# A hybrid attention and convolution layer on one core: x, weights, w_out and gates laid out in DRAM in the pieces in which they are loaded

## Chip, cores and metric

The kernel runs on one core of one Trainium2 chip. The metric is the device time of one execution in microseconds (us), lower is better.

## What is computed

One layer is applied to two sequences, of 256 and 2,048 tokens, each with the same 16 learned meta tokens ahead of it; the outputs of the meta tokens are dropped. All tensors are float32. Cut to what matters:

```python
h = rmsnorm(z, norm_w)                                  # z: (B, 16 + S, 1024)
proj = einsum('bld,de->ble', h, w_in)                   # w_in: (1024, 2816)
q, k, v, g_att, c_val, c_glu, g_conv = split(proj, ...) # 512 128 128 512 512 512 512
q, k = rmsnorm per head of 64                           # 8 query heads, 2 key heads
att = windowed_gqa(q, k, v, sink) * silu(g_att)         # window 128, ALiBi, meta keys, sink logit
u   = c_val * sigmoid(c_glu)
cnv = silu(layernorm(depthwise_conv31(u) + conv_b)) * silu(g_conv)
out = z + einsum('ble,ed->bld', concat([att, cnv]), w_out)
```

## The kernel before

**Precision.** Products are made from split operands: each float32 tensor becomes a rounded part and a remainder (`xh`, `xl` for x, the two halves of `ws` for the weights), and three matrix products stand in for one (`PASSES`, used at L763, L779 and L538).

**First part: projections.** The 2,304 tokens are 18 blocks of 128 and lie with 16 meta columns in six groups (`GROUPS`: one of 400 columns, five of 384). w_in is cut into 11 units of 256 columns: four for the convolution (GLU gate beside value), two convolution gates, two attention gates, one for k and v, two for q. The units are run over groups 0 to 2 first and over groups 3 to 5 after that. For each group `Prep` loads x transposed (`load`, L649, from `zt`, in four pieces of two row blocks each into `xt`), scales it (`scale`, L677) and splits it (`split`, L694 and L703). The scale needs the reciprocal norms, which `stats` makes from rows of z (L626 load, L632 squares, L122 and L123 the power) and `first` turns into a row with transposes (`bc`, L661). For each unit `weights` loads w_in in four pieces of 256 KB (L729, tile `wraw`), splits them (L738, L739) into `ws`, and for units after the second writes the split halves to DRAM (`wd`, L742), from where the second pass loads them (L720).

**What goes through DRAM between the parts.** The gates after SiLU (L871, tile `go`, three buffers) go to `gd`, queries to `qd`, keys to `kd`, values to `vd`, the convolution's output (made on VectorE at L846, one tap per instruction, beside the projections) to `cd`. `store` issues a store two ticks after its tile was made; a tick ends each half unit of a group.

**Second part: attention and output projection.** The 18 blocks are run in a pipeline of three stages with eight slots each (`slot_step`): scores of block a (L316, the bias and running maximum at L371, the exponential at L383), probabilities transposed and multiplied with v (L429, L464) for the block before, output projection (L538) for the one before that. `load_ga` (L299) and `load_mix` (L303, L305) bring the attention gate, the convolution gate and the convolution's output of a block; `merge` (L499, L505) and `mix_conv` (L515) multiply. `load_wo` (L290) loads w_out in 16 pieces of 256 KB through two `woraw` buffers, and `split_wo` (L294 on ScalarE, L295 on VectorE) splits them. This happens in the change-over, while the last q unit is still being projected.

**Order.** Nearly all transfers are issued by SyncE's one queue, in order. The scheduler orders the first part by a time model; in the second part GpSimd's order, and later TensorE's too, is that of the code (`manual_schedule`, `keep_in_program_order`). Each engine works through its instructions in order, so a waiting instruction holds those behind it.

Of the kernel before, what the change touches and what calls it, by code (L numbers as in the profile page):

```python
# [10 lines left out]
F32 = mybir.dt.float32  # L11
# [6 lines left out]
P = 128  # L18
D = 1024
ND = D // P  # L20
# [3 lines left out]
NB = NB_P + NB_S  # L24
TOK = NB * P
COLS = NM + TOK
# [6 lines left out]
UW = 256  # L33
# [27 lines left out]
GROUPS = [(0, 400)] + [(400 + 384 * i, 384) for i in range(5)]  # L61
# [14 lines left out]
def hymba_kernel(  # L76
# [13 lines left out]
    nc = tc.nc  # L90

    const = ctx.enter_context(tc.tile_pool(name="const", bufs=1, side="left"))
    dram = ctx.enter_context(tc.tile_pool(name="dram", bufs=1, space=bass.MemoryType.DRAM))
    psum = ctx.enter_context(tc.tile_pool(name="psum", bufs=2, space=bass.MemoryType.PSUM))

    qd = dram.tile([NB, P, 512], F32, name="qd")
    gd = dram.tile([8, P, TOK], F32, name="gd")
    kd = dram.tile([P, 2, KV, TOK], F32, name="kd")
    kmd = dram.tile([P, 2, KV, NM], F32, name="kmd")
    vd = dram.tile([NB, P, 2 * P], F32, name="vd")  # L100
# [35 lines left out]
    def later(k, f):  # L136
        due.setdefault(clock[0] + k, []).append(f)
# [20 lines left out]
    def store(dst, src):  # L158
        later(2, lambda: nc.sync.dma_start(dst, src))
# [53 lines left out]
    vt, qt, q2t, sbt, pmt, gat, gct, cnt, mix, att, yot, opj = ({} for _ in range(12))  # L213
# [45 lines left out]
    vt, qt, q2t, sbt, pmt, gat, gct, cnt, mix, att, yot, opj = ({} for _ in range(12))  # L259
# [17 lines left out]
    def load_wo(n):  # L277

        e = OUT_ORDER[n]
        for hl in range(2):  # L280
            idx = 2 * n + hl
            if idx % 3 == 0:
                slot = idx // 3
                wo_slot[slot] = xp.tile([P, ND, 400], F32R, tag=("xh", "xl")[slot % 2], name=f"wo{slot}")
            flat = wo_slot[idx // 3].rearrange("p a n -> p (a n)")
            wo[e, hl] = flat[:, D * (idx % 3) : D * (idx % 3) + D]
        for nh in range(2):
            cols = slice(512 * nh, 512 * nh + 512)
            raw = pool["a"].tile([P, 512], F32, tag="woraw", name=f"woraw{n}_{nh}", bufs=2)
            nc.sync.dma_start(raw, w_out[e][:, cols])  # L290
            later(2, lambda hi=wo[e, 0][:, cols], lo=wo[e, 1][:, cols], raw=raw: split_wo(hi, lo, raw))

    def split_wo(hi, lo, raw):
        nc.scalar.copy(hi, raw)  # L294
        nc.vector.tensor_tensor(lo, raw, hi, op=ALU.subtract)  # L295

    def load_ga(b):
        gat[b] = pool["b"].tile([P, 4, P], F32, tag="ga", name=f"ga{b}", bufs=1)
        nc.sync.dma_start(gat[b], gd[0:4, :, P * b : P * b + P].rearrange("j p n -> p j n"))  # L299

    def load_mix(b):
        gct[b] = pool["b"].tile([P, 4, P], F32, tag="gc", name=f"gc{b}")
        nc.sync.dma_start(gct[b], gd[4:8, :, P * b : P * b + P].rearrange("j p n -> p j n"))  # L303
        cnt[b] = pool["b"].tile([P, 4, P], F32, tag="cn", name=f"cn{b}")
        nc.sync.dma_start(cnt[b].rearrange("p j n -> p (j n)"), cd[b])  # L305

# [311 lines left out]
    if True:  # L618
# [20 lines left out]
        class Prep:  # L639
# [6 lines left out]
            def load(self, d2):  # L646
                n = self.n
                self.xt[d2] = sp.tile([P, 2, 400], F32, tag="xt", name=f"xt{self.g}_{d2}", bufs=XTB)
                nc.sync.dma_start(  # L649
                    self.xt[d2][:, :, :n],  # L650
                    zt[2 * d2 : 2 * d2 + 2, :, self.c0 : self.c0 + n].rearrange("d p n -> p d n"),
                )

            def first(self):
# [53 lines left out]
        def weights(k):  # L708

            key = keys[k]  # L710
            raw = {}

            def load(eng):
                pool = wl if k % 2 else wr
                ws = pool.tile([P, ND, 2, UW], F32R, tag="ws", name=f"ws{key[0]}_{key[1]}")
                wsplit[key] = ws
                if key[0] == 1 and key[1] >= CACHE:
                    for q in range(4):
                        part = ws[:, 2 * q : 2 * q + 2].rearrange("p d a n -> p (d a n)")
                        eng.dma_start(part.bitcast(F32), wd[key[1], q])  # L720
                    return
                for q in range(4):
                    if k == 1:
                        if q % 2 == 0:
                            pair = cp.tile([P, UWID], F32, tag="us", name=f"wraw{k}_{q}")
                        raw[q] = pair[:, 512 * (q % 2) : 512 * (q % 2) + 512].rearrange("p (a n) -> p a n", n=UW)
                    else:
                        raw[q] = sp.tile([P, 2, UW], F32, tag="wraw", name=f"wraw{k}_{q}", bufs=4)
                    dma = eng.dma_start(raw[q], w_in[key[1], :, 2 * q : 2 * q + 2, :])  # L729
                    if PIN_W <= k < 4:  # L730
                        tc.keep_in_program_order(dma)

            def split(q, eng):
                if key[0] == 1 and key[1] >= CACHE:
                    return
                ws = wsplit[key]
                hi, lo = ws[:, 2 * q : 2 * q + 2, 0, :], ws[:, 2 * q : 2 * q + 2, 1, :]
                nc.scalar.copy(hi, raw[q])  # L738
                eng.tensor_tensor(lo, raw[q], hi, op=ALU.subtract)  # L739
                if key[0] == 0 and key[1] >= CACHE:  # L740
                    part = ws[:, 2 * q : 2 * q + 2].rearrange("p d a n -> p (d a n)")
                    later(1, lambda: nc.sync.dma_start(wd[key[1], q], part.bitcast(F32)))  # L742

            return load, split

        pj_n = [0]
# [119 lines left out]
        def g_group(ws, t0, g):  # L866
            o = NM if g == 0 else 0
            for hi in range(2):
                ps = proj_et(ws, hi, g, o)
                so = gp.tile([P, 384], F32, tag="go", name=f"go{t0}_{hi}_{g}")  # L870
                nc.scalar.activation(so, ps[:, :384], AF.Silu)  # L871
                store(gd[t0 + hi, :, 384 * g : 384 * g + 384], so)
                tick(24 * 163)

        def head_norm(ps, rows, nh, tag):
# [168 lines left out]
        for i, (c, u, g) in enumerate(items):  # L1044
# [41 lines left out]
            if (c, u) == (0, ORDER[-1]):  # L1086
                p = preps[g + 3]
# [17 lines left out]
def layout(inputs):  # L1105
    f = {k: np.asarray(v) for k, v in inputs.items()}
    z = np.concatenate([f["meta_tokens"], f["x_prompt"][0], f["x_sample"][0]], axis=0)
    zt = np.ascontiguousarray(z.T).reshape(ND, P, COLS)
    w = f["w_in"][0]
    q, k, v, ga, cv, cg, gc = np.split(w, np.cumsum([512, 128, 128, 512, 512, 512])[:6], axis=1)  # L1110
    units = []
    for j in range(NJ):
        units.append(np.concatenate([cg[:, P * j : P * j + P], cv[:, P * j : P * j + P]], axis=1))
    units += [gc[:, :UW], gc[:, UW:], q[:, :UW], q[:, UW:], np.concatenate([k, v], axis=1), ga[:, :UW], ga[:, UW:]]
    w_in = np.stack([u.reshape(ND, P, UW).transpose(1, 0, 2) for u in units])
    col = lambda a, n: a.reshape(n, P).T
    vecs = np.concatenate(
        [
            col(f["norm_w"][0], 8),
            col(f["conv_b"][0], 4),  # L1120
            col(f["conv_ln_w"][0], 4),
            col(f["conv_ln_b"][0], 4),
            np.tile(f["q_norm_w"][0], 2)[:, None],
            np.tile(f["k_norm_w"][0], 2)[:, None],
        ],
        axis=1,
    )
    conv_w = f["conv_w"][0].reshape(TAPS, NJ, P).transpose(2, 1, 0)
    row = np.arange(P)
    local = row // QB  # L1130
    sink = np.stack([f["sink_logits"][0][4 * kv + local] for kv in range(KV)], axis=1)
    slopes = np.exp2(-8.0 * np.arange(1, H + 1, dtype=np.float32) / H).astype(np.float32)
    bias_c = np.zeros((P, KV, 4, SW), np.float32)
    for kv in range(KV):
        for n in range(4):
            col = QB * n + np.arange(SW)
            key = np.where(col < P, col - P, col - P - NM)
            dist = np.abs(key[None, :] - (QB * n + row % QB)[:, None]).astype(np.float32)
            full = np.where(dist <= P, slopes[4 * kv + local][:, None] * dist, np.float32(BIG))
            bias_c[:, kv, n] = np.where(((col >= P) & (col < P + NM))[None, :], np.float32(0.0), full)  # L1140
    mmask = ((np.arange(P)[:, None] // NM) % 4 == np.arange(4)[None, :]).astype(np.float32)
    w_out = f["w_out"][0].reshape(8, P, D)
    arrs = dict(z=z, zt=zt, w_in=w_in, w_out=w_out, vecs=vecs, conv_w=conv_w, sink=sink, bias_c=bias_c, mmask=mmask)
    return {k: np.ascontiguousarray(v) for k, v in arrs.items()}

# [16 lines left out]
```

## Time and profile before

| | |
|---|---|
| median of 3 runs | 978.2 us (976.36 to 978.36) |
| the profiled execution, own time | 976.89 us |
| span of its instructions | 975.1 us |
| TensorE matmul (PE) busy | 948.1 us, 97% |
| weight loads (PEld) busy | 885.9 us, 91% |
| VectorE (DVE) busy | 754.1 us, 77% |
| ScalarE (ACT) busy | 423.6 us, 43% |
| GpSimd (POOL) busy | 338.1 us, 35% |
| DMA | 155.75 MB in 113,872 packets, 160 GB/s in the mean |

The shares are averages over the parts of the program. Matmuls overlap in the profile, so a stretch in which PE is busy throughout has no gap, but says nothing of how far PE is from its peak. The granted clock is 1.00 at the full 2.4 GHz. A DMA's time is from its issue to its landing; the share of the DMA engines can read a little over 1 where they are full.

### The profile page before, as it was taken

To read this page: it belongs to the slowest core of one execution; us is meant where nothing else is said; L and a number is where in the kernel's file an instruction comes from. 1 tells how busy PE (TensorE), PEld (TensorE's weight loads), DVE (VectorE), ACT (ScalarE), POOL (GpSimd) and SP (SyncE) were. 2 spreads that over 40 slices of the span, in tenths; PEclk is the share of its full clock that TensorE was granted. 3 is DMA by queue.
4 is the path that set the end of the run, shared out by engine and by line. 5 is a ranking of instruction groups with operands and counts; after the bars stand their busy time and mean duration, and the time that the engine had idled before them with its cause. 6 is when DMAs were issued, how large, how long until landed. Compare 5 with 4: busy or idle time off the path is not lost.

```text
span 975.1 us, 16201 instructions
## 1 busy us (share of the span) xinstructions
PE 948.1 (97%) x5721; PEld 885.9 (91%) x5721; DVE 754.1 (77%) x1261; ACT 423.6 (43%) x1156; POOL 338.1 (35%) x541
## 2 busy tenths in 40 slices
PE   5999999999999999999999998899999999999998
PEld 4999999999999999999999998578888888888886
DVE  4659999998977799999983555977776777767772
ACT  6621121343566710111113454756665666666651
POOL 5600000354567300000002564645445543544451
PEclk9999999999999999999999999899999999999999
DMA  9653344775735222233335656954554455544321
GB/s 334 227 185 121 114 178 170 268 283 189 232 118 171 84 105 69 74 123 135 135 132 176 210 156 202 295 164 130 161 174 152 125 150 164 178 130 136 108 87 44
DMA packets 113872, 155.75 MB, mean 160 GB/s; under 512 B 10592, under 2 KB 77296, under 8 KB 113792
## 3 DMA queue, kind: packets, MB, share of 16 engines
q1 hardware_dynamic: 113648, 154.11, 48.0%
q0 software_dynamic: 144, 0.62, 0.4%
q8 instruction: 45, 0.74, 0.3%
q14 instruction: 35, 0.29, 0.1%
HBM read 101.00 MB, written 54.31 MB: 159 GB/s over the span
## 4 chain that ended last, share of the span: by engine, by line
PE 90%; DVE 4%; DMA 3%; POOL 1%; issue 1%; ACT 1%; SPq 0%; POOLq 0%; DVEq 0%; ACTq 0%
PE pj L763 42%; PE y L538 20%; PE pj L779 12%; PE O L464 5%; PE pT L429 4%; PE S L316 4%; DMA woraw<-in_w_out 1%; DMA snk<-in_sink 1%; PE O L316 1%; PE qT L316 1%; PE lnt L183 1%; DMA xn<-in_z 1%; DVE wo L295 1%; PE lnu L202 0%; DVE sb L371 0%
## 5 line engine op out<-in xcount | busy, mean ns | idle before, releaser
L763 PE MATMUL pj<-xh,ws 128*128 128x384 f32 (+1 forms) x1536 | 396.5, 339 | 2.4 <-ACT xh L694 2.4
L846 DVE SCALAR_TENSOR_TENSOR y<-us,cw,y 128x1167 f32<-128x1167 f32 x240 | 329.0, 1428 | 0.6
L763 PEld LDWEIGHTS pj<-xh,ws 128*128 128x128 f32 x1536 | 282.0, 189 | 2.7 <-ACT xh L694 2.7
L763 PE MATMUL pj<-xl,ws 128*128 128x384 f32 (+1 forms) x768 | 262.0, 341 | 0.0
L779 PE MATMUL pj<-ws,xh 128*128 128x256 f32 (+1 forms) x880 | 165.1, 285 | 0.5 <-DVE qs L899 0.5
L763 PEld LDWEIGHTS pj<-xl,ws 128*128 128x128 f32 x768 | 144.6, 188 | 1.0 <-DVE xl L703 0.8
L779 PEld LDWEIGHTS pj<-ws,xh 128*128 128x128 f32 (+1 forms) x880 | 136.9, 188 | 1.2 <-PE pj L779 0.6
L779 PE MATMUL pj<-ws,xl 128*128 128x256 f32 (+1 forms) x440 | 124.9, 284 | 0.0
L383 ACT ACTIVATE sb<-sb,nm 128x304 f32<-128x304 f32 (+4 forms) x144 | 77.1, 536 | 45.7 <-DVE nm L371 44.2
L538 PE MATMUL y<-wo,mch 128*128 128x512 f32 x288 | 96.7, 417 | 0.0
L538 PE MATMUL y<-wo,mah 128*128 128x512 f32 x288 | 94.1, 407 | 0.7 <-DVE wo L295 0.4
L441 DVE TENSOR_TENSOR pl<-pT,ph 128x512 fp32r<-128x512 f32 x100 | 69.0, 690 | 30.0 <-ACT ph L440 29.5
L871 ACT ACTIVATE go<-pj 128x384 f32<-128x384 f32 x48 | 23.6, 491 | 152.9 <-PE pj L763 144.4
L371 DVE CUSTOM_DVE_ANT_0 sb<-S,bias,nsnk 128x304 f32<-128x304 f32 (+4 forms) x144 | 73.5, 511 | 14.8 <-PE S L316 14.5
L779 PEld LDWEIGHTS pj<-ws,xl 128*128 128x128 f32 (+1 forms) x440 | 82.8, 188 | 0.2
L122 POOL TENSOR_SCALAR ssk<-ssk 128x2 f32<-128x2 f32 x18 | 6.4, 356 | 210.9 <-ACT sqk L885 210.8
L440 ACT CAST ph<-pT 128x512 fp32r<-128x512 f32 x100 | 58.2, 583 | 42.2 <-PE pT L429 41.5
L406 POOL TENSOR_SCALAR sb<-sb,es 128x304 f32<-128x304 f32 (+4 forms) x144 | 72.5, 523 | 3.5
L316 PEld LDWEIGHTS S<-kw,q 128*128 128x128 f32 x288 | 53.7, 190 | 18.2 <-DVE nm L371 6.3
L316 PE MATMUL S<-kw,q 128*128 128x304 f32 (+4 forms) x288 | 62.6, 299 | 5.7 <-DVE nm L371 5.7
L122 POOL TENSOR_SCALAR ssq<-ssq 128x4 f32<-128x4 f32 (+2 forms) x55 | 25.0, 454 | 118.6 <-ACT xn L632 78.6
L429 PE MATMUL pT<-ident,sb 128*128 128x128 f32 x400 | 62.5, 276 | 1.8 <-POOL sb L406 1.6
(118 smaller groups left out, 1434.1 us busy)
## 6 DMA issues: line engine op xcount, KB each, us to landing
wd<-ws SPq DMA_DIRECT2D x36, 512.0 KB, 5.5
ws<-wd SPq DMA_DIRECT2D x36, 512.0 KB, 6.2
wraw<-in_w_in SPq DMA_DIRECT2D x52, 256.0 KB, 6.1
xn<-in_z SPq DMA_DIRECT2D x18, 512.0 KB, 5.8
gd<-go SPq DMA_DIRECT2D x48, 192.0 KB, 2.1
yo<-in_z SPq DMA_DIRECT2D x36, 256.0 KB, 2.7
out_y<-yo SPq DMA_DIRECT2D x36, 256.0 KB, 2.1
kw<-kd SPq DMA_DIRECT2D x16, 512.0 KB, 5.6
```

The lines of the kernel that those rows point to most:

```text
L316: r = f(*a, **k)
L371: nc.vector.tensor_tensor_reduce(out=sb[:, n, c0:c1], in0=ps[:, 0:w], in1=cst["bias"][:, kv, n, c0 - QB * n : c1 - QB * n], scale=1.0, sca ...
L383: nc.scalar.activation(sb[:, n, c0:c1], sb[:, n, c0:c1], AF.Exp, bias=nm[:, n : n + 1], scale=-1.0, accum_out=rs[:, n : n + 1],)
L406: nc.gpsimd.tensor_scalar(sb[:, k, a0:a1], sb[:, k, a0:a1], es[:, k : k + 1], 1.0, op0=ALU.mult, op1=ALU.mult)
L429: nc.tensor.transpose(pt[:, hl, :], sbt[b, kv][:, hl, KCOL[k] : KCOL[k] + P], ident)
L440: nc.scalar.copy(ph, pt)
L441: nc.vector.tensor_tensor(pl, pt, ph, op=ALU.subtract)
L464: nc.tensor.matmul(o, lhs, t, start=(start and i == 0), stop=(stop and i == 1))
L538: nc.tensor.matmul(ps, mh[mi][:, e % 4, :], wo[e, wi][:, cols], start=(e == 4 and k == 0), stop=(e == 3 and k == 2),)
L763: nc.tensor.matmul(ps[:, :n], ws[:, d, wi, P * half_i : P * half_i + P], x[xi][:, d, o : o + n], start=(k == 0), stop=(k == 3 * ND - 1),)
L779: nc.tensor.matmul(ps[:rows, :UW], x[xi][:, d, o : o + rows], ws[:, d, wi, :], start=(k == 0), stop=(k == 3 * ND - 1),)
L846: nc.vector.scalar_tensor_tensor(y[:, yo + o0 : yo + o1], u[:, o0 + k : o1 + k], cw[:, j, k : k + 1], y[:, yo + o0 : yo + o1], op0=ALU.mul ...
```

## The change

Four tensors get another order in DRAM; every load and store keeps its place and its bytes. The inputs are laid out on the host, outside the timed part.

- `zt`: the columns of x stood as [8, 128, 2320], and a piece took 400 or 384 columns out of two row blocks. Now the pieces stand one behind the other, each [128, 2, n].
- `w_in`: a unit stood as [128, 8, 256], and a piece took 2 KB of each partition's 8 KB. Now a unit is four blocks of [128, 2, 256].
- `w_out`: a row block stood as [128, 1024], and a piece took 2 KB of each 4 KB. Now it is two blocks of [128, 512].
- `gd`: the gates stood as [8, 128, 2304], a store wrote 384 columns of a partition in one run, and a load took four runs of 128 columns. Now they stand as [18, 128, 8, 128]: a store writes three runs of 128 columns, a load takes one run of 512.

```diff
-    gd = dram.tile([8, P, TOK], F32, name="gd")
+    gd = dram.tile([NB, P, 8, P], F32, name="gd")
...
-            nc.sync.dma_start(raw, w_out[e][:, cols])
+            nc.sync.dma_start(raw, w_out[e, nh])
...
-        nc.sync.dma_start(gat[b], gd[0:4, :, P * b : P * b + P].rearrange("j p n -> p j n"))
+        nc.sync.dma_start(gat[b], gd[b, :, 0:4])
...
-        nc.sync.dma_start(gct[b], gd[4:8, :, P * b : P * b + P].rearrange("j p n -> p j n"))
+        nc.sync.dma_start(gct[b], gd[b, :, 4:8])
...
                 self.xt[d2] = sp.tile([P, 2, 400], F32, tag="xt", name=f"xt{self.g}_{d2}", bufs=XTB)
+                o = P * (ND * self.c0 + 2 * d2 * n)
                 nc.sync.dma_start(
-                    self.xt[d2][:, :, :n],
-                    zt[2 * d2 : 2 * d2 + 2, :, self.c0 : self.c0 + n].rearrange("d p n -> p d n"),
+                    self.xt[d2][:, :, :n], zt[o : o + 2 * P * n].rearrange("(p d n) -> p d n", p=P, d=2)
                 )
...
-                    dma = eng.dma_start(raw[q], w_in[key[1], :, 2 * q : 2 * q + 2, :])
+                    dma = eng.dma_start(raw[q], w_in[key[1], q])
...
-                store(gd[t0 + hi, :, 384 * g : 384 * g + 384], so)
+                store(
+                    gd[3 * g : 3 * g + 3, :, t0 + hi].rearrange("b p n -> p b n"), so.rearrange("p (b n) -> p b n", n=P)
+                )
...
-    zt = np.ascontiguousarray(z.T).reshape(ND, P, COLS)
+    zc = z.T.reshape(4, 2, P, COLS)
+    zt = np.concatenate([zc[q, :, :, c : c + n].transpose(1, 0, 2).ravel() for c, n in GROUPS for q in range(4)])
...
-    w_in = np.stack([u.reshape(ND, P, UW).transpose(1, 0, 2) for u in units])
+    w_in = np.stack([u.reshape(4, 2, P, UW).transpose(0, 2, 1, 3) for u in units])
...
-    w_out = f["w_out"][0].reshape(8, P, D)
+    w_out = f["w_out"][0].reshape(8, P, 2, 512).transpose(0, 2, 1, 3)
```

Every engine has the same instructions in the same order as before, and each waits for the same semaphores; rows differ in their forms alone. On SyncE's queue at the start of the program, where the first group of x and the first unit of w_in are loaded (the numbers behind the names count tiles, those behind x are partitions and the rest of a transfer's shape; line numbers behind an added line are shifted):

```order
-L987 DMA vec<-in_vecs 128x22
-L649 DMA xt_0_116<-in_zt 128x2x400
-L649 DMA xt_1_118<-in_zt 128x2x400
+L989 DMA vec<-in_vecs 128x22
+L650 DMA xt_0_116<-in_zt 128x800
+L650 DMA xt_1_118<-in_zt 128x800
 L729 DMA wraw_0_121<-in_w_in 128x512
 L729 DMA wraw_1_123<-in_w_in 128x512
 L729 DMA wraw_2_125<-in_w_in 128x512
 L729 DMA wraw_3_127<-in_w_in 128x512
```

Nothing moved; the loads of the 400 columns became one run per partition, and those of w_in, already one run of 2 KB, kept their form. Loads of 384 columns keep two runs, since a row of `xt` is 400 long:

```order
-L649 DMA xt_0_213<-in_zt 128x2x384
-L649 DMA xt_1_217<-in_zt 128x2x384
-L649 DMA xt_2_221<-in_zt 128x2x384
-L649 DMA xt_3_225<-in_zt 128x2x384
+L650 DMA xt_0_213<-in_zt 128x2x384
+L650 DMA xt_1_217<-in_zt 128x2x384
+L650 DMA xt_2_221<-in_zt 128x2x384
+L650 DMA xt_3_225<-in_zt 128x2x384
```

They stand where they stood, in the same form. On the same queue in the change-over, where the first gates (`ga`, `gc`) are loaded among the pieces of w_out (`woraw`):

```order
 L159 DMA qd<-qs_15_6346 128x256
 L290 DMA woraw_1_6302<-in_w_out 128x512
-L299 DMA ga_6573<-gd 128x4x128
-L303 DMA gc_6575<-gd 128x4x128
+L299 DMA ga_6573<-gd 128x512
+L303 DMA gc_6575<-gd 128x512
 L290 DMA woraw_0_6305<-in_w_out 128x512
 L159 DMA qd<-qs_16_6432 128x256
 L305 DMA cn_6577<-cd 128x512
 L290 DMA woraw_1_6307<-in_w_out 128x512
-L303 DMA gc_6592<-gd 128x4x128
+L303 DMA gc_6592<-gd 128x512
```

Again nothing moved; the gate loads became one run per partition.

## Rows read from the trace of the kernel before

**Rows 1.** Stretches: length, busy PE, PEld, DVE, ACT, POOL (count); clock, DMA share, GB/s.

```profile
...
0.00:16.40 16.40, 5.31 (x14) 3.72 (x15) 5.86 (x10) 9.97 (x18) 6.85 (x17) 1.00 0.88 308
16.40:290.00 273.60, 273.60 (x1745) 271.85 (x1744) 237.89 (x275) 98.60 (x293) 84.97 (x106) 1.00 0.57 196
290.00:307.00 17.00, 15.92 (x132) 15.27 (x131) 12.03 (x23) 11.64 (x58) 14.31 (x22) 1.00 0.59 175
307.00:590.00 283.00, 283.00 (x1845) 282.86 (x1844) 228.03 (x258) 76.81 (x202) 49.40 (x117) 1.00 0.38 128
590.00:655.00 65.00, 53.98 (x304) 44.61 (x303) 46.86 (x125) 40.01 (x109) 35.00 (x53) 0.92 0.76 234
655.00:957.00 302.00, 302.00 (x1632) 256.14 (x1632) 219.05 (x566) 185.23 (x475) 146.48 (x228) 1.00 0.45 138
...
```

**Rows 2.** Waits of PE over the whole span: total us, times, longest us.

```profile
...
PE bc L661 <- POOL rstd L123: 8.7, 4, 4.9
PE S L316 <- DVE nm L371: 5.7, 2, 4.5
PE pj L763 <- ACT xh L694: 2.4, 1, 2.4
...
```

**Rows 3.** Instructions in time in the head: start, us, in brackets the idle time before.

```profile
...
10.44 2.26 DVE L677 SCALAR_TENSOR_TENSOR xt<-xt,vec,bc 128x400 f32<-128x400 f32 x4 [2.22 <-PE bc L661]
11.66 0.62 ACT L738 CAST ws<-wraw 128x512 fp32r<-128x512 f32 x1 [2.70 <-DMA wraw<-in_w_in]
12.19 0.95 ACT L694 CAST xh<-xt 128x400 fp32r<-128x400 f32 x2
...
```

**Rows 4.** Chain of waits in the change-over: start, us, what.

```profile
...
592.58 5.58 DMA woraw<-in_w_out
...
606.76 3.76 DMA woraw<-in_w_out
...
611.92 4.34 DMA woraw<-in_w_out
...
```

**Rows 5.** DMA of 633 to 634: packets and their sizes; queue, packets, MB, busy share.

```profile
...
DMA packets 479, 0.26 MB, mean 257 GB/s; under 512 B 19, under 2 KB 465, under 8 KB 479
...
q1 hardware_dynamic: 479, 0.26, 85.7%
...
```

**Rows 6.** The same of 49 to 50.

```profile
...
DMA packets 274, 0.40 MB, mean 398 GB/s; under 512 B 15, under 2 KB 274, under 8 KB 274
...
q1 hardware_dynamic: 274, 0.40, 106.6%
...
```

**Rows 7.** Busy time of two stretches in the head, columns as in rows 1.

```profile
...
9.00:11.00 2.00, 0.56 (x2) 0.18 (x1) 0.56 (x2) 0.00 (x0) 0.73 (x2) 1.00 0.87 222
11.00:12.00 1.00, 0.00 (x0) 0.00 (x0) 1.00 (x3) 0.34 (x1) 0.00 (x0) 1.00 1.04 397
...
```

**Rows 8.** The gate tiles go: ACT's idle time before them, and store to landing.

```profile
...
  PE pj L763: 144.4, 40
...
DMA to landing us min/median/max: 1.8/2.1/8.3
```

**Rows 9.** DMA issues of the whole run: count, KB each, median us to landing.

```profile
...
yo<-in_z SPq DMA_DIRECT2D x36, 256.0 KB, 2.7
...
kd<-ks SPq DMA_DIRECT2D x18, 256.0 KB, 2.6
...
ga<-gd SPq DMA_DIRECT2D x18, 256.0 KB, 4.0
...
woraw<-in_w_out SPq DMA_DIRECT2D x16, 256.0 KB, 3.7
...
```

**Rows 10.** Busy time of three stretches of the change-over, columns as in rows 1.

```profile
...
600.00:610.00 10.00, 10.00 (x72) 10.00 (x73) 7.70 (x24) 7.17 (x21) 7.21 (x11) 0.83 0.58 172
620.00:630.00 10.00, 7.86 (x26) 4.92 (x27) 9.85 (x24) 7.25 (x19) 8.18 (x11) 0.70 1.02 330
630.00:640.00 10.00, 10.00 (x54) 8.48 (x53) 7.96 (x22) 6.82 (x18) 5.03 (x8) 0.96 0.67 210
...
```
## The prediction

> **What bounds the kernel now.** First the busy time by stretches [rows 1]. TensorE (PE) is busy all 273.60 us from 16.4 to 290, all 283.00 us from 307 to 590 and all 302.00 us from 655 to 957. Outside the last 18 us it is idle in three places only: 11.1 us in the head (16.40 - 5.31), 1.1 us at 290 to 307, and 11.0 us in the change-over from the projections to the attention, 590 to 655 (65.00 - 53.98). A faster transfer can shorten the span only where PE waits in the end for a transfer; in the three full stretches, 858.6 us together, it cannot.
>
> Second, what PE waits for [rows 2]. No wait of PE names a DMA. In the head it waits 8.7 us for the reciprocal norms (bc on rstd) and 2.4 us for the first rounded x (xh). In the change-over the longest single wait is 4.5 us, on a VectorE (DVE) maximum.
>
> Third, the step behind those waits. In the head the first scaled half of xt is ready about 0.57 us after 10.44 (a quarter of 2.26 us), but ScalarE (ACT), which runs in order, first has to cast a weight piece; it stood 2.70 us for wraw until 11.66 and so casts xh only at 12.19 [rows 3]. In the change-over the chain of waits goes through three loads of woraw, of 5.58, 3.76 and 4.34 us [rows 4]: ACT's cast of a w_out piece stands in its order ahead of the exponentials and squares, so a late woraw holds those up, and PE behind them. These are the two places where a load of a kind that the change touches reaches PE.
>
> Fourth, what a transfer costs by the size of its pieces, in stretches that hold one kind. 633 to 634 is nearly all a gate load in 512 B pieces (0.26 MB in 479 packets): 257 GB/s at 85.7% busy, so 300 GB/s were the 16 engines full [rows 5]. 49 to 50 is x in 1,536 B pieces (0.40 MB in 274): 398 at 106.6%, 373 [rows 6]. At 11 to 12 it is w_in in 2 KB pieces that lie 8 KB apart: 397 at 1.04, 382. At 9 to 11 pieces of w_in ran at 222 GB/s at 0.87 [rows 7].
>
> **The change, part by part.** No instruction moves on any engine; only source, target and piece sizes of transfers differ, so the terms are transfer times.
>
> *w_in (52 loads of 256 KB) and w_out (16).* The pieces stay 2 KB to a partition; only their distance falls, from 8 KB and 4 KB to 2 KB. By the 382 GB/s above, at a distance of 8 KB, there is nothing left to gain against other 2 KB pieces. Bounds: nothing, and what a prompt wraw could save in the head, at most 1.2 us (xh at 12.19 against the 11.0 at which its input is ready [rows 3]). I take 0: the nearest row with the same tensor at full flow is the one at 382 [rows 7].
>
> *Columns of x (24 loads).* Each source is now one block, but a tile's rows in SBUF are 400 columns long, and five of the six groups have 384. So the 20 loads of those groups still move two pieces of 1,536 B to a partition, and only the four of the first group become 128 pieces of 3,200 B. Two of these stand ahead of the first wraw: 819,200 B at 373 GB/s are 2.20 us, at 382 they are 2.14. I take 0.1 us off the head; the bounds are those of the head, 0 to 1.2.
>
> *Gate stores (48).* 128 pieces of 1,536 B become 384 of 512 B: 196,608 B take 0.53 us of all engines at 373 and 0.66 at 300, so each costs 0.13 us more, 6.2 us in all. They lie in the stretches where PE never waits. The cover is the go buffers: a store lands in 2.1 us in the middle, 8.3 at worst, and ACT has waited 144.4 us in 40 waits for PE before its SiLUs [rows 8]. A tile therefore comes at most every 3.6 us, the store is issued two such steps later, and three buffers last three of them: a landing up to 3.6 us holds up nobody. Over that ACT first uses up the 3.6 us that it waits anyway, and PE has four more accumulators (tags a and b, two buffers each). Cost: 0. The bound on the other side is a landing that grows as the stores of k do, which already go in 512 B pieces: 256 KB in 2.6 us, against 2.1 for the 192 KB of a gate store [rows 8, 9]. That is still inside the 3.6 us.
>
> *Gate loads (18 ga, 18 gc).* 512 pieces of 512 B become 128 of 2 KB: 262,144 B fall from 0.87 us to 0.69 (at 300 and 382 GB/s), 0.19 us each. From 655 on, PE has no idle time [rows 1], so nothing comes of it there; the loads just land earlier. In the change-over ga0, gc0 and gc1 are queued among the woraw loads that ACT waits for, on engines that are busy 0.76 of that stretch [rows 1]. If all three count, that is 0.56 us; I take 0.5. Bounds: 0, and all that PE idles there, 11.0 us, plus the clock. The clock: after idle time PE was granted 0.83 of full speed at 600 to 610 and 0.70 at 620 to 630 [rows 10], each a mix of the two levels 2.4 and 1.2 GHz, with 0.96 at 630 to 640, so 1.7 and 3.0 + 0.4 us of work lost. No row supports more than a part of that.
>
> The Trainium skill, DMA: Bandwidth & Descriptors, section Specifications, asks for at least 512 B in a piece for line rate, which speaks against a gain from these loads: by it 512 B and 2 KB would cost the same and the sum would be 0.1 us. The trace disagrees, 300 GB/s against 382 [rows 5, 7].
>
> **The sum.** 0.1 + 0.5 = 0.6 us off the profiled execution. That one took 976.89 us, 1.3 under the median of the three runs, 978.2 (976.36 to 978.36). With that execution as a fourth, the mean is 977.5; less 0.6 that is 976.9, rounded to 977.0. A measurement of this kernel can tell about 0.2%, 2 us, from no change; I forecast less than that.
>
> **The rivals.**
>
> *Distant pieces are slow in themselves.* For it: 222 GB/s at 9 to 11 on w_in [rows 7], and woraw's 3.7 us in the middle against yo's 2.7 at equal size [rows 9]. Against it: the same w_in pieces at 382 a moment later, and yo, which also takes 2 KB out of rows of 4 KB. If it held, the first wraw would come early enough to save the 1.2 us of the head. In the change-over 222/0.87 = 255 would become 382, so the pair of woraw (524,288 B) at the first link would be 0.7 us sooner and the two single ones 0.3 each, 1.3 in all. That is 2.5, and with the gate loads 3.1. If the shorter waits also spare PE the slow clock at 600 to 610 or at 620 to 640, 1.7 or 3.4 more. From 976.89 that gives 973.8 down to 970.4. Chance 0.27. The Trainium skill, same page, section Latency and other measured facts, has this as a rule: a row pitch at a large power of two slows a copy, and tiles are better laid out contiguously. Its figures begin at 512 KiB, far over the pitches here, and no run here shows it.
>
> *Slower: the change-over starts sooner and then stands longer.* From 620 to 630 DVE is busy 9.85 of 10 us [rows 10]. Earlier loads let PE run ahead into that stretch, where it waits for DVE in one longer piece; if its clock then falls while the dense work from 630 on is due (PE is busy 10.00 of 10 there), a slow stretch like the one at 620 to 640 costs 3.4 us more. With the 0.6 gained that is 979.7. It decides if the low clock lies behind 630 instead of mostly ahead of it. For it speaks that the clock fell twice in this stretch; against it, that shorter waits should make it fall less. Chance 0.10.
>
> *The change does not do what it says.* For 20 of the 24 loads of x no piece grows, and none does for w_in and w_out. If the gate loads are hidden too, the time stays: 976.9 on this execution. That is inside the forecast.
>
> **How the numbers follow.** Forecast and no effect together 0.63, distant pieces 0.27, slower 0.10. Of the first, a tenth may fall out on either side by the scatter of the runs alone, mostly on the fast side where the bounds are wide: 0.05 faster, 0.02 slower. Faster by over 0.2%: 0.27 + 0.05 = 0.32. Slower: 0.10 + 0.02 = 0.12. Same: 0.56. The range runs from 972.5, the middle of the first rival's span, to 979.7, where the slower rival lands.
>
> **What would show it.** Right: ga lands in under 3.5 us, against 4.0 [rows 9]; gd stores stay under 3.6 us in the middle; PE still full from 16.4 to 290, 307 to 590 and 655 to 957; PE's first projection starts between 12.3 and 12.8 us. The first rival shows as a start of that projection before 11.9, full flow at 9 to 11 and woraw in under 3 us; the slower one as a stretch of half clock after 630. Wrong altogether: any wait of PE in the projection stretches, or a change of over 3 us that lies outside the head and the change-over.

## The result and the profile after

| | before | after |
|---|---|---|
| median, lowest to highest of 20 runs each | 977.87 us, 975.91 to 979.74 | 978.77 us, 977.48 to 980.16 |
| profiled execution, span | 976.89, 975.1 | 979.33, 977.5 |

The ratio, worked out over all runs, is 1.0014 with a 95% interval of 1.0008 to 1.0020: the change makes the kernel 0.14% slower, 0.8 to 2.0 us (the medians alone differ by 0.90 us). The forecast was 0.6 us the other way.

The busy time by stretches after the change (length, then PE, PEld, DVE, ACT and POOL busy with their counts, then clock, DMA share, GB/s):

```profile
0.00:16.40 16.40, 3.99 (x10) 2.46 (x11) 6.49 (x10) 10.06 (x18) 8.13 (x18) 1.00 0.90 335
16.40:290.00 273.60, 273.60 (x1734) 272.61 (x1733) 238.00 (x271) 96.77 (x286) 84.39 (x102) 1.00 0.56 194
...
307.00:590.00 283.00, 283.00 (x1845) 282.86 (x1844) 228.74 (x256) 75.33 (x201) 49.05 (x119) 1.00 0.40 128
590.00:655.00 65.00, 54.52 (x309) 46.09 (x307) 47.49 (x128) 40.62 (x109) 33.89 (x50) 0.89 0.74 232
655.00:957.00 302.00, 301.49 (x1629) 255.85 (x1630) 218.36 (x565) 185.50 (x477) 147.89 (x232) 1.00 0.44 140
...
9.00:11.00 2.00, 0.47 (x1) 0.18 (x1) 0.86 (x2) 0.71 (x2) 0.54 (x1) 1.00 1.05 398
11.00:12.00 1.00, 0.62 (x2) 0.50 (x2) 1.00 (x3) 0.98 (x3) 0.05 (x1) 1.00 1.06 399
...
620.00:630.00 10.00, 7.01 (x29) 4.40 (x29) 9.85 (x26) 8.14 (x22) 8.16 (x11) 0.89 1.02 331
630.00:640.00 10.00, 10.00 (x47) 8.52 (x46) 7.13 (x16) 4.95 (x13) 6.22 (x9) 0.77 0.63 216
```

Against [rows 1], the two projection stretches are as full as they were; from 655 to 957 PE idles 0.51 us, where before it idled none. PE lost time in the head: 3.99 us busy instead of 5.31. Yet the loads there got better: 9 to 11 us ran at 398 GB/s, against 222 [rows 7].

The waits of PE over the whole span (total us, times, longest us):

```profile
PE bc L661 <- POOL rstd L123: 8.4, 4, 5.0
PE S L316 <- DVE nm L371: 5.6, 2, 4.4
PE pj L763 <- DVE xl L703: 2.7, 1, 2.7
...
PE pj L763 <- ACT xh L694: 1.3, 1, 1.3
```

Against [rows 2], the wait for xh went from 2.4 us to 1.3, as an earlier first weight piece should make it. But a wait that was not there before stands in its place: 2.7 us for xl, the part that rounding leaves over, from DVE.

Two pieces of the head in order of time show where it comes from (start, us, in brackets the idle time before). First the changed kernel:

```profile
10.14 2.26 DVE L677 SCALAR_TENSOR_TENSOR xt<-xt,vec,bc 128x400 f32<-128x400 f32 x4 [2.23 <-PE bc L661]
10.29 0.62 ACT L738 CAST ws<-wraw 128x512 fp32r<-128x512 f32 x1 [1.62 <-DMA wraw<-in_w_in]
...
10.81 1.06 ACT L694 CAST xh<-xt 128x400 fp32r<-128x400 f32 x2
...
11.38 1.03 PE L763 MATMUL pj<-xh,ws 128*128 128x400 f32 x2 [1.28 <-ACT xh L694]
...
11.95 1.04 POOL L703 TENSOR_TENSOR xl<-xt,xh 128x400 fp32r<-128x400 f32 x1 [2.38 <-ACT xh L694]
...
12.31 1.23 DVE L739 TENSOR_TENSOR ws<-wraw,ws 128x512 fp32r<-128x512 f32 x1
...
12.95 1.72 POOL L739 TENSOR_TENSOR ws<-wraw,ws 128x512 fp32r<-128x512 f32 x1
...
14.62 1.39 POOL L703 TENSOR_TENSOR xl<-xt,xh 128x400 fp32r<-128x400 f32 x1
...
15.15 0.70 PE L763 MATMUL pj<-xl,ws 128*128 128x400 f32 x1 [2.74 <-DVE xl L703]
...
18.66 0.87 PE L763 MATMUL pj<-xh,ws 128*128 128x400 f32 x2
...
19.32 0.87 PE L763 MATMUL pj<-xl,ws 128*128 128x400 f32 x2
```

Then the kernel before:

```profile
12.61 0.68 DVE L739 TENSOR_TENSOR ws<-wraw,ws 128x512 fp32r<-128x512 f32 x1
...
12.76 1.04 PE L763 MATMUL pj<-xh,ws 128*128 128x400 f32 x2 [2.36 <-ACT xh L694]
...
13.21 1.47 POOL L703 TENSOR_TENSOR xl<-xt,xh 128x400 fp32r<-128x400 f32 x1 [3.34 <-ACT xh L694]
13.21 0.57 DVE L703 TENSOR_TENSOR xl<-xt,xh 128x400 fp32r<-128x400 f32 x1
...
13.84 0.70 PE L763 MATMUL pj<-xl,ws 128*128 128x400 f32 x1
...
18.59 0.34 PE L763 MATMUL pj<-xh,ws 128*128 128x400 f32 x1
...
18.77 0.34 PE L763 MATMUL pj<-xl,ws 128*128 128x400 f32 x1
```

ACT's first weight cast starts 1.37 us earlier (10.29 against 11.66 in [rows 3]), xh 1.38 (10.81 against 12.19), PE's first projection matmul 1.38 (11.38 against 12.76). DVE gains only 0.3 us: its scaling of xt waits for the norms (`bc`), not for the weights, and is done at 12.40 instead of 12.70. (Over all the profiles below it starts at 9.95 to 10.21 us with the new order of w_in and at 10.07 to 10.51 with the old one.) Before, POOL's half of xh was ready at 13.14, when DVE was nearly done with its weight piece (13.29). Now both halves of xh are ready at 11.87, while DVE is still scaling, and POOL begins its subtraction ahead of DVE's weight piece. Both engines run instructions with two inputs in SBUF, and they slow each other: DVE's weight piece takes 1.23 us instead of 0.68, and its first xl, for which PE's third matmul waits, 1.65 instead of 0.57. The chain in the head has that one by itself (start, us, what):

```profile
12.39 0.49 DVE ws L739
12.89 0.58 issue
13.46 1.65 DVE xl L703
15.11 0.04 issue
15.15 3.04 PE pj L763 x8
```

So PE starts 1.38 us earlier and has its third operand 1.31 us later (15.15 against 13.84). To that comes the slow clock. At first one matmul of 400 columns follows the next at 0.33 us (two from 18.66 to 19.32), later at 0.18 (18.59, 18.77). f4 below has the 0.33 us where its granted clock is recorded as 0.50, so that is the lower level, 1.2 GHz, and the other is 2.4. In the kernel before the step is at 16.4 us, after the change at 20.2: there 18 to 20 us still touches 8 matmuls, where before it touched 13.

The loads and stores by kind (count, KB each, median us to landing), for [rows 8] and [rows 9]:

```profile
gd<-go SPq DMA_DIRECT2D x48, 192.0 KB, 2.4
...
ga<-gd SPq DMA_DIRECT2D x18, 256.0 KB, 3.9
...
woraw<-in_w_out SPq DMA_DIRECT2D x16, 256.0 KB, 3.3
```

### The profile page after: what moved, and what is told of

It reads as the page before. It is cut to its first block, busy times and chain, and to the rows that moved or that the text cites. A ratio compares the mean times of both kernels' runs of the same rounds, so it can differ in the third digit from the quotient of the medians.

```text
span 977.5 us, 16201 instructions
## 1 busy us (share of the span) xinstructions
PE 949.2 (97%) x5721; PEld 888.5 (91%) x5721; DVE 756.5 (77%) x1261; ACT 423.6 (43%) x1156; POOL 339.2 (35%) x541
## 4 chain that ended last, share of the span: by engine, by line
PE 90%; DVE 4%; DMA 3%; POOL 1%; ACT 1%; issue 1%; SPq 0%; POOLq 0%; ACTq 0%
PE pj L763 42%; PE y L538 20%; PE pj L779 12%; PE O L464 5%; PE pT L429 4%; PE S L316 4%; DMA woraw<-in_w_out 1%; DMA snk<-in_sink 1%; PE O L316 1%; PE lnt L183 1%; PE lnu L202 1%; PE qT L316 1%; DVE wo L295 1%; DMA xn<-in_z 1%; DVE sb L371 0%
```

## The experiments

The theory: **turns in the head**. The new order of w_in alone makes the first weight piece earlier, this lets POOL go ahead of DVE, and the slower DVE costs more than the earlier start gives. Its rivals: the gate stores in pieces of 512 B cost time that is hidden in no wait of PE; or the change-over does it, by the clock that falls into dense work. All were timed against the kernel before on the same chip: e1 to e4 on one (before: 977.12 us), f1 to f4 on another (977.26).

This table holds what each profile shows of the head: GB/s from 5 to 10 us, the start of PE's first and third projection matmul, and the PE instructions that fall into 12 to 22 us. At the full rate one follows the next at 0.18 us.

| run | median us | ratio, 95% interval | GB/s | first | third | matmuls |
|---|---|---|---|---|---|---|
| before, as profiled | 977.87 | 1 | 359 | 12.76 | 13.84 | 39 |
| after, as profiled | 978.77 | 1.0014, 1.0008 to 1.0020 | 400 | 11.38 | 15.15 | 27 |
| e1 w_in alone | 978.68 | 1.0016, 1.0007 to 1.0025 | 393 | 11.60 | 15.25 | 25 |
| e2 all but w_in | 977.40 | 1.0002, 0.9992 to 1.0011 | 349 | 12.35 | 14.33 | 34 |
| e3 gates alone | 977.19 | 1.0000, 0.9991 to 1.0009 | 358 | 12.57 | 14.76 | 29 |
| e4 after, head relieved | 976.49 | 0.9994, 0.9985 to 1.0003 | 403 | 11.39 | 13.55 | 36 |
| f1 after again | 978.99 | 1.0019, 1.0010 to 1.0028 | 393 | 11.49 | 15.19 | 29 |
| f2 as e4, again | 977.16 | 0.9998, 0.9989 to 1.0007 | 405 | 11.31 | 13.47 | 40 |
| f3 before, head relieved | 976.66 | 0.9997, 0.9989 to 1.0006 | 355 | 12.84 | 13.67 | 37 |
| f4 as e4, PE busy early | 974.38 | 0.9976, 0.9966 to 0.9986 | 405 | 11.71 | 12.74 | 46 |

**e1: the kernel before, with the order of w_in alone.**

```diff
-                    dma = eng.dma_start(raw[q], w_in[key[1], :, 2 * q : 2 * q + 2, :])
+                    dma = eng.dma_start(raw[q], w_in[key[1], q])
...
-    w_in = np.stack([u.reshape(ND, P, UW).transpose(1, 0, 2) for u in units])
+    w_in = np.stack([u.reshape(4, 2, P, UW).transpose(0, 2, 1, 3) for u in units])
```

> The kernel before with w_in alone laid out in blocks. Theory head: the early weight pieces land sooner, ScalarE casts the first one near 10.3 us instead of 11.7, GpSimd's split of x starts near 12 and VectorE's own first split of x then runs beside GpSimd work and takes over 1.2 us instead of 0.57; the third projection matmul starts near 15.1 instead of 13.8, full clock comes later than 16.4, and the time is 1 to 2 us over the kernel before (ratio 1.001 to 1.002). Theory gates (three-piece stores cost) and theory change-over (new timing of ga, gc and woraw costs): ratio 1.000, since neither is in this kernel.

It is as slow as the whole change, 1.0016 against 1.0014, and its head is the same (in order of time):

```profile
12.05 1.04 POOL L703 TENSOR_TENSOR xl<-xt,xh 128x400 fp32r<-128x400 f32 x1 [2.41 <-ACT xh L694]
...
12.38 1.25 DVE L739 TENSOR_TENSOR ws<-wraw,ws 128x512 fp32r<-128x512 f32 x1
...
15.25 0.70 PE L763 MATMUL pj<-xl,ws 128*128 128x400 f32 x1 [2.62 <-DVE xl L703]
```

POOL is ahead of DVE, DVE's piece takes 1.25 us, and PE waits 2.62 us for xl. The loss comes with w_in.

**e2: the change with w_in as before.**

```diff
-                    dma = eng.dma_start(raw[q], w_in[key[1], q])
+                    dma = eng.dma_start(raw[q], w_in[key[1], :, 2 * q : 2 * q + 2, :])
...
-    w_in = np.stack([u.reshape(4, 2, P, UW).transpose(0, 2, 1, 3) for u in units])
+    w_in = np.stack([u.reshape(ND, P, UW).transpose(1, 0, 2) for u in units])
```

> The changed kernel with w_in put back as it was; x, w_out and the gates stay changed. Theory head: the first weight cast waits until over 11 us again, the third projection matmul starts near 13.8, ratio 1.000 or up to 0.001 below. Theories gates and change-over: the loss stays, ratio 1.001 to 1.002.

The other three tensors together are worth nothing that can be measured, 1.0002, and the first weight piece is late again: ACT's cast starts at 11.25 us. But the third matmul, expected near 13.8 us, starts at 14.33. Here too POOL's xl stands ahead of DVE's, by 0.05 us, and 1.48 us pass from the start of DVE's to the matmul that waits for it, against 0.63 in the kernel before:

```profile
12.80 1.04 POOL L703 TENSOR_TENSOR xl<-xt,xh 128x400 fp32r<-128x400 f32 x1 [3.30 <-ACT xh L694]
...
12.85 3.00 DVE L703 TENSOR_TENSOR xl<-xt,xh 128x400 fp32r<-128x400 f32 x2
```

**e3: the kernel before, with the order of the gates alone** (the lines of `gd` in the diff above).

```diff
-    gd = dram.tile([8, P, TOK], F32, name="gd")
+    gd = dram.tile([NB, P, 8, P], F32, name="gd")
...
-                store(gd[t0 + hi, :, 384 * g : 384 * g + 384], so)
+                store(
+                    gd[3 * g : 3 * g + 3, :, t0 + hi].rearrange("b p n -> p b n"), so.rearrange("p (b n) -> p b n", n=P)
+                )
```

> The kernel before with the gates alone laid out by block (stores in three pieces of 512 B, loads in one of 2 KB). Theory gates: ratio 1.001 to 1.002, with waits of ScalarE or TensorE in 120 to 225 or 410 to 517 us. Theory head: ratio 1.000, PE full in both stretches. Theory change-over: between the two, with the difference at 600 to 640.

1.0000: 48 stores in three times as many pieces, and 36 loads in a quarter of them, come to nothing. Its profiled execution (979.16 us, the longest of its 12) shows something else, in order of time:

```profile
13.03 1.25 POOL L703 TENSOR_TENSOR xl<-xt,xh 128x400 fp32r<-128x400 f32 x1 [3.08 <-ACT xh L694]
...
14.76 0.70 PE L763 MATMUL pj<-xl,ws 128*128 128x400 f32 x1 [1.15 <-DVE xl L703]
```

Here, with the old order of w_in, POOL's xl starts 0.26 us ahead of DVE's at 13.29 (in the kernel before both stand at 13.21), and PE gets its third operand 0.92 us later than in the profile of before. So with the old order too POOL's xl can come first: it does in two of three profiles (e2 and e3, not before), and the third matmul starts at 13.84, 14.33 and 14.76 us. With the new order it does in all three (after, e1, f1), and there POOL also catches DVE's weight piece, which takes 1.23 to 1.25 us instead of 0.68 or 0.69. Then the third matmul starts between 15.15 and 15.25.

**e4 and f2: the change, with POOL out of the way of DVE.** In the first group, DVE also makes the second xl and the second weight piece, which POOL had.

```diff
-                        eng = nc.gpsimd if dd else nc.vector
+                        eng = nc.gpsimd if dd and (self.g or d2) else nc.vector
...
-            w01[0][1](q, nc.gpsimd if q % 2 else nc.vector)
+            w01[0][1](q, nc.gpsimd if q == 3 else nc.vector)
```

> The changed kernel, but in the head VectorE instead of GpSimd makes the first remainder of x beside its own and the second weight piece, so that GpSimd does nothing until VectorE has made what the third matmul needs. Theory head: the third projection matmul starts at 13.2 to 13.6 instead of 15.1, and the time falls by 1.5 to 3 us against the changed kernel, to 0.998 to 1.000 of the kernel before. Theories gates and change-over: ratio stays at 1.001 to 1.002.

```profile
12.32 0.68 DVE L739 TENSOR_TENSOR ws<-wraw,ws 128x512 fp32r<-128x512 f32 x1
...
12.92 1.05 DVE L703 TENSOR_TENSOR xl<-xt,xh 128x400 fp32r<-128x400 f32 x2
...
13.55 0.70 PE L763 MATMUL pj<-xl,ws 128*128 128x400 f32 x1 [1.12 <-DVE xl L703]
...
13.85 2.72 POOL L703 TENSOR_TENSOR xl<-xt,xh 128x400 fp32r<-128x400 f32 x1 [4.27 <-ACT xh L694]
...
13.89 0.68 DVE L739 TENSOR_TENSOR ws<-wraw,ws 128x512 fp32r<-128x512 f32 x1
...
14.49 0.57 DVE L703 TENSOR_TENSOR xl<-xt,xh 128x400 fp32r<-128x400 f32 x1
...
14.98 0.68 DVE L739 TENSOR_TENSOR ws<-wraw,ws 128x512 fp32r<-128x512 f32 x1
```

With the same transfers as the changed kernel, DVE's two xl take 1.05 us together, less than the first alone took beside POOL (1.65), and the third matmul starts at 13.55. The loss is gone: 0.9994.

> The changed kernel once more, to see whether its head repeats and to stand beside the next three on one chip. Theory head: the third projection matmul starts again near 15.1 us, after two that start near 11.4, and the ratio is 1.001 to 1.002. Theory scatter (the head seen before was one execution's luck): the third matmul starts elsewhere, 13.8 to 15.1, and the ratio is nearer to 1.000.

f1 is the changed kernel, unaltered, timed beside f2 on the same chip: 1.0019, with the same head.

> The changed kernel with GpSimd out of the way in the head, repeated beside it. Theory head: third matmul near 13.5 us, 1.5 to 2.5 us faster than the changed kernel on the same chip (ratio to the kernel before 0.999 to 1.000). Rival: the 0.9994 seen was scatter and it stands at 1.001.

f2 is e4 again: 0.9998 with 1.0007 as its upper end, where f1 begins at 1.0010. The same edit takes 0.2% off the changed kernel.

**f3: the kernel before, with the edit of e4.**

> The kernel before, all layouts old, with the same reassignment in the head. It tells what the earlier landing of w_in is worth once nothing is in VectorE's way. Theory head: ScalarE still waits for the first weight piece until about 11.6, the third matmul starts at 13.6 to 14.0, so this kernel is 0 to 0.4 us slower than the same reassignment on the new layout and 0 to 0.5 us faster than the kernel before (0.9995 to 1.000). Rival (the layout is worth nothing or costs even so): it is faster than the new layout with the same reassignment.

0.9997, against 0.9998 for f2. With POOL out of the way the order in DRAM makes no difference that can be measured: f2 starts its first projection 1.53 us earlier (11.31 against 12.84), but the third matmul, which waits for DVE, only 0.20 (13.47 against 13.67). f3 was expected 0 to 0.4 us above f2 and came out 0.50 below it, which is inside the noise. Whoever wanted to use the earlier weights would have to make DVE earlier too. And the edit itself gives the old kernel nothing that stands clear of the noise, though e2 and e3 suggested that it might.

What the head costs in sum shows in a matmul far behind it. Counted in the traces, the 1,000th of the projections starts at 194.76, 195.04 and 194.77 us where the order is new and POOL in the way (after, e1, f1), at 193.00, 193.81 and 194.42 where the order is old (before, e2, e3), and at 193.15, 192.40 and 192.84 where POOL is out of the way (e4, f2, f3).

**f4: e4, with PE kept busy in the first 8 us** by 40 transposes of the identity, whose result nobody reads. They stand ahead of the loads in the program and wait for `ident` alone.

```diff
+        wps = psum.tile([P, 512], F32, tag="d", name="wps")
+        for i in range(WARM):
+            nc.tensor.transpose(wps[:, P * (i % 4) : P * (i % 4) + P], ident, ident)
         nc.sync.dma_start(vec, vecs)
```

> The changed kernel with the reassignment and, from 1.3 us on, 40 transposes of the identity whose result nobody reads, ahead of the first real matmul. It tells what the half clock after the start costs: in the kernel with the reassignment alone the matmuls run at half clock for about 5 us after the third one starts. Theory clock: they run at full clock from the start or soon after, which is worth 1 to 2.5 us against the reassignment alone (ratio 0.997 to 0.9985). Rival (in the first 8 us the matmuls are held by the splits, not by the clock): within 0.5 us of the reassignment alone.

The stretches of its head, columns as above:

```profile
0.00:5.30 5.30, 3.94 (x19) 3.94 (x20) 0.07 (x1) 3.05 (x5) 1.43 (x8) 1.00 0.58 201
5.30:8.00 2.70, 2.70 (x25) 2.50 (x23) 0.16 (x1) 2.41 (x5) 1.27 (x4) 1.00 1.03 403
8.00:11.70 3.70, 0.92 (x4) 0.34 (x3) 1.75 (x4) 1.71 (x5) 1.01 (x3) 1.00 1.05 399
...
12.15:15.56 3.41, 3.05 (x10) 2.70 (x9) 3.41 (x8) 2.35 (x5) 1.51 (x1) 0.50 1.04 400
15.56:20.00 4.44, 4.44 (x26) 4.44 (x26) 3.41 (x6) 3.94 (x9) 4.29 (x6) 1.00 1.03 394
```

It beats both kernels: 0.9976, 974.38 us. The clock rose during the transposes: 19 PE instructions took 3.94 us before 5.3, 25 took 2.70 after it. It was still full for the first two projection matmuls, which take 0.68 us together instead of e4's 1.03, fell to half at 12.15 after the little work of 8 to 11.7, and was full again from 15.56 on. At the half clock four matmuls begin from 13.58 to 14.91 us, 0.33 us each. From 12 to 22 us 46 matmuls fall against f2's 40, about 1.1 us of the 2.2 between their ratios.

But f4 is not f2 with a warm clock alone. With the transposes in the program, the scheduler put other instructions of the head in another order: ACT casts the first xh (10.61 us) ahead of the first weight piece (11.04), and DVE makes its first xl ahead of its weight piece:

```profile
12.12 0.57 DVE L704 TENSOR_TENSOR xl<-xt,xh 128x400 fp32r<-128x400 f32 x1
...
12.61 0.68 DVE L740 TENSOR_TENSOR ws<-wraw,ws 128x512 fp32r<-128x512 f32 x1
```

So the third matmul starts at 12.74 us, 0.73 ahead of f2's, and for that DVE's order is the reason, not the clock. What the clock alone is worth is not shown. Nor is the rest settled: in its profile PE is also busy 56.44 us of 590 to 655, where f2's has 55.37. It was not tried on the old order of the tensors either; that the gain does not depend on the new one is argued from f2 and f3, not shown.

## Why the prediction was wrong

**What bounds the kernel: right.** The stretches of the projections stayed full [rows 1], and the loss that the experiments find came out of the head, one of the two places named.

**Gate stores: right.** Taken as 0 under the waits before the SiLUs [rows 8]; they land in 2.4 us, under 3.6, and e3 measured 1.0000.

**Gate loads and w_out: over-rated.** The 0.5 us rested on loads that land sooner. ga lands in 3.9 us, not under 3.5, woraw in 3.3 instead of 3.7, and not under 3 as the first rival wanted; in the middle of other traffic the size of the pieces hardly shows. e2, which has both, measured 1.0002, so 0.5 us (0.05%) is inside its interval, but nothing speaks for it.

**Columns of x: not told apart.** 0.1 us is below what e2 can tell.

**w_in: the step that failed.** It was taken as 0, because the tensor ran at 382 GB/s at 11 to 12 us [rows 7], and bounded by "nothing, and what a prompt wraw could save in the head, at most 1.2 us". Both halves were wrong, and so was the premise behind them, that no instruction moves and the terms are thus transfer times: none moves in its engine's own order, but two engines changed places against each other. The row that decided was the other one of that group: the 222 GB/s fell on the very loads that ACT waits for, and with whole blocks they ran at 398. So the first rival was right on its first half: flow at 9 to 11, first projection before 11.9 us. But the bound excluded a loss without a reason, and it followed one chain only, ACT's cast, xh, PE. Behind the first two matmuls stands a second chain, DVE's scaling, weight piece and xl, that the load doesn't shorten; and the load is also what held POOL back. The rows had the reason in view [rows 3]: DVE is scaling until 12.70, xh's second half was ready at 13.14, so POOL came when DVE's weight piece was nearly done. Moving ACT by 1.4 us and DVE by 0.3 put POOL ahead of that piece. In the profiled pair this makes the third matmul late by 1.31 us, over the three profiles of each order by 0.4 to 1.4; e1 puts the whole loss there by the tensor, e4 and f2 by the engines.

**The slower rival: its place was wrong.** It put the loss into the change-over, by a clock that falls into dense work after 630. In the profiled execution this is seen, 0.77 at 630 to 640 against 0.96 [rows 10], but f2, with the same transfers, has 0.93 there and f3, with the old ones, 0.89, and f2's ratio is the same as f3's within the noise. It varies between executions and was not shown to be part of the difference.

**The size.** 978.77 us lies inside the range of 972.5 to 979.7; the sign was wrong. (The lower end was to be the middle of the first rival's span, 973.8 to 970.4; that middle is 972.1.) The profiled pair differs by 2.44 us, more than the 0.8 to 2.0 of the ratio. From 12 to 22 us the changed kernel has 12 matmuls less, 2.2 us at 0.18 each; the 1.31 us of the late operand are in that, and the half clock that lasts longer. At the 1,000th matmul 1.76 us of it are left, and the remaining 0.7 come later in that pair. And the forecast held 2 us for the least that can be told from no change; with 20 runs of each kernel the interval is 1.2 us wide, so that a loss of 1.4 stands clear of it.

## What to carry to other kernels

A load that comes earlier is a change of order among the engines that it releases: list all of them, and ask which will now start ahead of which. Before a faster transfer is priced, follow the second and third operand of the waiting instruction as well as the first; a gain ends where the next chain stands. And where two engines share work on a critical stretch, time one of them with the other idle before splitting it.

## What was not expected of the hardware

**DVE and POOL took turns, whole instructions long.** In the changed kernel POOL's xl ends at 12.99 (11.95 + 1.04), and DVE's weight piece, in progress since 12.31, ends 0.55 us later. POOL's weight piece ends at 14.67 (12.95 + 1.72), and DVE's xl 0.44 later, at 15.11. POOL's next xl (14.62 + 1.39) ends 0.90 after that. In e4 POOL's xl ends at 16.57, 0.91 us after the last of the three DVE instructions that ran since it began (14.98 + 0.68). The other engine's share of its time is thus not half speed but a wait for the end of the instruction ahead, and then nearly its own time: 0.55 of 0.68, 0.44 of 0.57, 0.90 of 1.04.

The Trainium skill, SBUF — State Buffer, section Who interferes with whom, says that a VectorE instruction with two SBUF inputs contends with a GpSimd instruction that reads SBUF, that the ports they share are an exclusive lock, and that the order of issue decides who blocks. With the lock the trace agrees at all the ends above. The order of issue holds where POOL began at 11.95, but not in e4: there POOL is recorded from 13.85 and stood through DVE instructions that began at 13.89, 14.49 and 14.98. The record doesn't show what decides the next turn.

**The same 2 KB pieces, at 8 KB distance, ran at 222 GB/s early and 397 a microsecond later** [rows 7]; laid out in one block, at 398 and 399. From 5 to 10 us all six profiles with the new w_in have 393 to 405 GB/s, the four with the old one 349 to 359. By the landings in the traces only the first piece of w_in is late: with the old order it comes 1.42 to 1.90 us after the x ahead of it, the next three 0.65 to 0.79 after one another; with the new order it takes 0.68, about as long as the others. Why only the first one is slow was not tried.

**The clock column says 1.00 from 12 to 18 us in the changed kernel, where matmuls follow each other at half the rate**; f4, whose clock rose and fell earlier, has 0.50 in its rows. The first record of the clock in the trace stands at 20.2 us there and at 16.4 in the kernel before. Ahead of it the spacing of equal matmuls tells the clock, and the column doesn't.
